# A feed-forward product in seven block products instead of eight, its weight sums made by accumulating DMAs, and the residual kept in DRAM

## The chip, the cores and the metric

The kernel runs on one core of one Trainium2 chip. The metric is the device time of one execution in microseconds (us); less is better. Engines are named as the profile names them: PE (TensorE, the matmuls), DVE (VectorE), ACT (ScalarE), POOL (GpSimd), SP (SyncE, which issues DMAs here).

## What is computed

One layer of a hybrid encoder block on 512 positions plus 16 learned meta positions, with 1024 channels, then a final RMSNorm. The part that the change touches is the feed-forward at the end:

```python
D_MODEL, SEQ, D_FF, FFN_CONV_K = 1024, 512, 2816, 3
...
    h = h + (g_conf * y_conf + g_dn * y_dn) @ w_out
    u2 = rmsnorm(h, norm_ffn_w)
    up = causal_dwconv(u2 @ w_up, ffn_dw_w, ffn_dw_b)
    f_gate, f_val = jnp.split(up, 2, axis=-1)
    return h + (jax.nn.silu(f_gate) * f_val) @ w_down
```

Ahead of it stand a projection `u @ w_in`, a convolution branch, and a gated delta rule with 8 heads in 4 chunks. `u2 @ w_up` has an inner size of 1024 and 5632 output channels: 22 tiles of 128 gate channels and 22 of value channels.

## The kernel before

Everything is float32. A product of full precision is made of three passes: weight and activation are each split into a high part (float32r, a rounded form) and a low part (the rest), and high x high, high x low and low x high are added in PSUM. `weights` loads a 128x1024 weight tile into one of three `wr` buffers by an SP DMA, ACT casts it to `wh`, DVE subtracts to get `wl` (two buffers each). `gemm` issues the matmuls: for 128 output channels and two halves of about 258 positions (256 and two of overlap for the convolution) 8 inner tiles x 3 passes x 2 halves = 48 matmuls of 258 columns.

The stages, in time: the norm and the keys of the heads; the convolution branch; the inverses of the heads' small triangular matrices, which DVE makes in 32x32 blocks and `grow` puts together with 32- and 64-row matmuls on PE (tiles `gP`, `gX`, with `LL` as an operand that POOL clears first); the heads' chunk chains mixed with the products `q`, `v`, `z`, `ga`; the products `y` and `wo`; then the feed-forward. There `up(t)` makes the product of one tile of 128 channels, DVE multiplies it by the norm's reciprocal root `r2` as it leaves PSUM (two instructions of 258 columns), ACT and DVE apply the three taps, ACT the SiLU, DVE multiplies gate by value and both split the result for the second product (tiles `dn`), which starts when the 44th `up` is done. The residual stays in eight SBUF tiles `hs` from `wo` to the end. Big temporary tiles come from a pool of 75 buffers, `bt`.

The order of the instructions of each engine is fixed by a list scheduler that runs when the program is built (`Plan.order`): each recorded operation has a priority (its place in the recording, moved by entries of a table `BIAS`), a modelled cost and its dependencies. Each engine then runs its own list strictly in order and waits at semaphores. So an instruction that waits holds up all behind it on its engine. POOL's list holds only 8 masks (`AFFINE_SELECT`, for tiles `E`) and small `MEMSET`s: of `LL`, and of the four pad columns of `ra`, the copy of `q` or `v` that the short convolution of each head reads. SP issues all DMAs.

Of the kernel before, what the change touches and what calls it, by code (L numbers as in the profile page):

```python
# [36 lines left out]
ROW = T + PAD  # L37

# [82 lines left out]
class Op:  # L121
    _fields = ("eng", "fn", "a", "k", "prio", "deps", "succ", "late", "wait", "cost", "ready", "end", "tiles", "lat", "table", "mode", "act", "tail", "alone")
# [21 lines left out]
TURN = {(False, True): 92, (True, False): 105, (True, True): 190}  # L144
# [6 lines left out]
STAY = 750  # L151
SWITCH = 600

BIAS = {'iv': -1500, 'd0': 100, 'v4': 40, 'v2': 100, 'z1': -570, 't11': -280, 't7': 350, 'k0': -70, 'ln': 250, 's7': -320, 'z0': -700, 'o2': 100, 'o5': 1600, 'd5': -650, 'g3': 150, 'd1': 2160, 'k2': -30, 'q7': -1720, 'k5': -30, 's4': -830, 'w3': -3100, 't2': -670, 'c5': -130, 't8': -40, 'o4': -350, 'q6': 350, 'g4': -350, 't4': -350, 'o1': 250, 'q4': -60, 't9': -750, 'z2': -600, 'o0': -600, 'g0': 30, 'q3': 500, 'q5': 100, 'c6': -30, 's1': -130, 't15': -100, 't1': -730, 's3': -470, 'y0': 250, 't12': -150, 'o6': 700, 'o3': -500, 'k4': -100, 'w2': 250, 't5': -150, 'v0': 30, 'g6': -120, 'z3': 250, 'g5': -190, 'q2': -70, 'y7': -30, 's5': -70, 'v6': -100, 'g1': -250, 'g7': 250, 'm4': 100, 'q0': -250, 'c7': -130, 'd3': -1750, 'o7': 100, 'm6': 30, 'm1': 30, 's6': -100, 'd2': -100, 'y6': 70, 'g2': -600, 'k6': -30, 'z4': -500, 't6': 100, 't3': 250}
LNP = 74
IVP = 1295
UP = 519
WP = 30
# [23 lines left out]

AFTER = 24
# [3 lines left out]
PARTS = (slice(1, 3), slice(0, 1))  # L187

# [9 lines left out]
class Plan:  # L198
# [18 lines left out]
    def add(self, eng, fn, a, k):  # L217
# [28 lines left out]
        if eng == "PE" and fn == "matmul":  # L246

            up = lambda n: 32 if n <= 32 else 64 if n <= 64 else P
            o.mode = (up(args[1].shape[0]), up(writes[0].shape[0]))
            o.mode = None if o.mode == (P, P) else o.mode  # L250
        o.cost, o.lat = self.price(eng, fn, a, k, writes[0])
        o.alone = self.price(eng, fn, a, k, writes[0], True)[0] if o.mode else o.cost
# [11 lines left out]
    def price(self, eng, fn, a, k, out, alone=False):  # L264
        n = out.n
        if eng == "PE":
# [4 lines left out]

            if out.ap.offset // out.tl.row and not alone:
                return 22, 0
# [3 lines left out]
            if lhs.shape[0] == 64:  # L277
                return 115, 0
            return max(n, lhs.n) / 0.6 + 8, 0
        if fn == "dma_start":  # L280
            return 475, int(np.prod(out.shape)) * 4 / 290.0 * (1 if self.run(k) >= P else 2)
# [10 lines left out]
    def order(self):  # L292
# [16 lines left out]
        table, dma, low, done = None, 0.0, 0, bytearray(len(ops))  # L309
        win, act, cold = 0, 0.0, True  # L310
        mode = None
# [14 lines left out]
        def look(e, t):  # L326

            q, nxt, best = ready[e], later[e][0][0] if later[e] else None, None
            for p, i in q:
# [26 lines left out]
                if e == "PE" and mode and o.mode != mode:  # L356
                    p += STAY
                elif o.table and table not in o.table:
                    p += SWITCH
# [4 lines left out]
        while len(out) < len(ops):  # L364
# [26 lines left out]
            if e == "PE":  # L391

                while t >= (win + 1) * WIN:
                    if act < LOW * WIN:
                        cold = True
                    elif act > HIGH * WIN:
                        cold = False
                    win, act = win + 1, 0.0
                if o.mode != mode:
                    c = o.alone + TURN[bool(mode), bool(o.mode)]  # L400
                if cold:
                    c *= 2
                act += o.act * (2 if cold else 1)
                mode = o.mode
            free[e] = t + c
            o.end = free[e]
# [43 lines left out]
def record(A, out):  # L450
# [52 lines left out]
    def gemm(acc, ws, ah, al, ranges, k0=0, kn=None, first=True, last=True):  # L503
# [275 lines left out]
    def decays(h):  # L779
# [54 lines left out]

    ivt = {}
# [350 lines left out]
    r2v = []  # L1186
# [8 lines left out]
    def up(t):  # L1195
# [17 lines left out]
    for t in range(FT):  # L1213
        g = up(t)
# [6 lines left out]
    cuts = ((0, 8), (8, 8), (16, 6))  # L1221

# [5 lines left out]
    for f in range(KT - 1):  # L1228
# [3 lines left out]
        o = hs[f]  # L1232
# [9 lines left out]
    o, s = hs[f], bt(n="fsq")  # L1242
    for b in range(2):
# [50 lines left out]

def _cols(v):
# [43 lines left out]
```

## Time and profile before

| | |
|---|---|
| median of 3 runs | 1037.63 us (1037.09 to 1038.33) |
| the profiled execution, its own time | 1037.14 us, span 1035.4 us, 1.7 us around it |
| PE busy | 1019.7 us, 98% of the span |
| DVE, ACT, POOL busy | 717.1 us, 476.7 us, 8.4 us |
| mean granted TensorE clock | 0.989 of full speed |
| DMA | 98.4 MB, a mean of 95 GB/s |

Busy time is the union of the instructions' own durations. Matmuls overlap (one lasts some 280 ns, the next starts 120 ns after it), so work on PE is counted by start-to-start times, not by durations.

### The profile page before, as it was taken

Reading aid. Unit: us, or ns where it says so; the run is one execution under the profiler, and the core shown is the slowest. Engines: PE = TensorE matmul, PEld = TensorE weight load, DVE = VectorE, ACT = ScalarE, POOL = GpSimd, SP = SyncE. Lnnn points to the kernel's source line nnn. Section 1 sums busy time; section 2 is a strip of 40 time slices with the busy share of each in tenths; the row PEclk is TensorE's granted clock in tenths of the full one; section 3 lists DMA queues with packets and bytes.
Section 4 is the critical chain, followed back from the end, with each engine's and each line's share of the span. In section 5 each row is a group of like instructions: output and inputs, shape, how many; then the busy total and the mean of one; then the engine's idle time right before and its main releaser. Section 6 shows DMA issues by size and latency. Waiting matters only on the chain.

```text
span 1035.4 us, 20014 instructions
## 1 busy us (share of the span) xinstructions
PE 1019.7 (98%) x8430; PEld 978.8 (95%) x8430; DVE 717.1 (69%) x1237; ACT 476.7 (46%) x847; POOL 8.4 (1%) x45
## 2 busy tenths in 40 slices
PE   9999999998999999999999999999999999999996
PEld 7999999998999999999999999999999999988886
DVE  5985699996599999996266555667676767623323
ACT  5787622446645565453254233544444444422222
POOL 0000000000000000000000000000000000000000
PEclk9999999997999999999999999999999999999998
DMA  6143333241121241214214332222222222333332
GB/s 220 63 135 93 100 108 111 83 123 52 43 97 54 67 132 54 93 62 144 82 42 153 115 121 82 86 100 83 101 86 99 82 103 84 95 92 92 97 92 82
DMA packets 44042, 98.40 MB, mean 95 GB/s; under 512 B 12720, under 2 KB 19248, under 8 KB 43952
## 3 DMA queue, kind: packets, MB, share of 16 engines
q1 hardware_dynamic: 43952, 97.12, 28.7%
q8 instruction: 66, 1.08, 0.4%
q14 instruction: 24, 0.20, 0.1%
HBM read 93.89 MB, written 3.21 MB: 94 GB/s over the span
## 4 chain that ended last, share of the span: by engine, by line
PE 92%; DVE 3%; ACT 3%; DMA 1%; issue 1%; SPq 0%; POOL 0%; DVEq 0%; ACTq 0%; POOLq 0%
PE up L447 25%; PE dn L447 12%; PE ga L447 9%; PE y L447 9%; PE z L447 5%; PE v L447 5%; PE wo L447 5%; PE q L447 4%; PE cv L447 4%; PE cg L447 3%; PE k L447 2%; PE o L447 2%; PE rs L447 1%; PE S L447 1%; PE wP L447 1%; DVE cv L447 1%
## 5 line engine op out<-in xcount | busy, mean ns | idle before, releaser
L447 DVE TENSOR_TENSOR wl<-wr,wh 128x1024 fp32r<-128x1024 f32 x157 | 189.3, 1206 | 156.7 <-PE dn L447 59.8
L447 ACT CAST wh<-wr 128x1024 fp32r<-128x1024 f32 x157 | 162.6, 1037 | 250.2 <-PE dn L447 57.5
L447 DVE SCALAR_TENSOR_TENSOR ca<-c,par,ca 128x516 f32<-128x516 f32 (+13 forms) x240 | 175.5, 742 | 3.1 <-ACT ca L447 0.3
L447 PE MATMUL up<-hh,wh 128*128 128x258 f32 x704 | 141.6, 282 | 0.0
L447 PE MATMUL up<-hl,wh 128*128 128x258 f32 x704 | 141.3, 282 | 0.0
L447 PEld LDWEIGHTS up<-hh,wh 128*128 128x128 f32 x704 | 109.2, 190 | 0.2 <-issue 0.2
L447 PEld LDWEIGHTS up<-hl,wh 128*128 128x128 f32 x704 | 108.7, 189 | 0.0
L447 PE MATMUL up<-hh,wl 128*128 128x258 f32 x704 | 91.9, 283 | 0.0
L447 PEld LDWEIGHTS up<-hh,wl 128*128 128x128 f32 x704 | 87.5, 190 | 0.0
L447 PE MATMUL dn<-fh,wh 128*128 128x512 f32 (+1 forms) x198 | 71.7, 370 | 0.0
L447 PE MATMUL dn<-fl,wh 128*128 128x512 f32 (+1 forms) x198 | 71.2, 368 | 0.0
L447 DVE SCALAR_TENSOR_TENSOR uy<-up,par,uy 128x512 f32<-128x512 f32 x88 | 65.9, 749 | 2.8 <-ACT uy L447 1.3
L447 DVE TENSOR_TENSOR up<-up,r 128x258 f32<-128x258 f32 x88 | 33.5, 420 | 47.1 <-PE up L447 44.3
L447 ACT ACTIVATE uy<-up,par 128x512 f32<-128x512 f32 x44 | 35.9, 816 | 55.4 <-DVE up L447 55.4
L447 PE MATMUL ga<-uh,wh 128*128 128x258 f32 (+1 forms) x256 | 56.9, 287 | 0.0
L447 PE MATMUL ga<-ul,wh 128*128 128x258 f32 (+1 forms) x256 | 56.6, 288 | 0.0
L447 DVE SCALAR_TENSOR_TENSOR cv<-ra,par,cv 128x528 f32<-128x528 f32 x69 | 51.3, 759 | 0.2
L447 PE MATMUL dn<-fh,wl 128*128 128x512 f32 (+1 forms) x198 | 45.4, 369 | 0.0
L447 PE MATMUL ga<-uh,wl 128*128 128x258 f32 (+1 forms) x256 | 44.6, 289 | 0.0
L447 PEld LDWEIGHTS dn<-fh,wh 128*128 128x128 f32 x198 | 37.2, 188 | 7.0
L447 PEld LDWEIGHTS dn<-fl,wh 128*128 128x128 f32 x198 | 37.2, 188 | 6.6
L447 PEld LDWEIGHTS ga<-uh,wh 128*128 128x128 f32 x256 | 42.1, 190 | 0.2
(284 smaller groups left out, 2195.9 us busy)
## 6 DMA issues: line engine op xcount, KB each, us to landing
wr<-in_win SPq DMA_DIRECT2D x64, 512.0 KB
wr<-in_wup SPq DMA_DIRECT2D x44, 512.0 KB
wr<-in_wd SPq DMA_DIRECT2D x17, 512.0 KB
wr<-in_wdn SPq DMA_DIRECT2D x8, 512.0 KB
wr<-in_wco SPq DMA_DIRECT2D x8, 512.0 KB
wr<-in_wo SPq DMA_DIRECT2D x8, 512.0 KB
wr<-in_wd SPq DMA_DIRECT2D x8, 384.0 KB
x<-in_xT SPq DMA_DIRECT2D x8, 264.0 KB
```

The source lines that it names most:

```text
L447: getattr(engines[o.eng], o.fn)(*(get(x) for x in o.a), **{n: get(x) for n, x in o.k.items()})
```

## The change

The feed-forward's first product is made for 3 of its 22 tile pairs (gate tile t and value tile t) as before. The other 19 pairs, called blocks here, are each a 2x2 block product: two halves of the inner size, two halves of the output channels (gate, value), two halves of the positions. `seven` makes it with seven block products in place of eight, in Winograd's form, which shares sums: each product has 4 inner tiles x 3 passes = 12 matmuls of 258 columns, and the seven accumulate in two PSUM regions X and Z whose running value is taken out between products (`quarters`: four takes by ACT, three by DVE).

- The sums of activations are made once, by `factors`, for the four pairs of inner tiles, right after `r2`: DVE first multiplies the residual by norm weight and `r2` (tiles `xn`; so the blocks need no multiplication by `r2` later), makes the sums (`nt`, `nq`) and splits all seven operands (`nh`, `nl`, `nhl`).
- The sums of weights are made by `presums` in DRAM, one 1 MB tile `ws` for each block: POOL issues two copies DRAM to DRAM of 512 KB and three accumulating DMAs (512, 256 and 256 KB). Accumulating ones wait for those before. Two blocks are under way at a time, and the first waits for the last mask.
- Each block's weights come in 3 loads of 512 KB and one of 256 KB, each split by ACT and DVE, in place of two of 512 KB.
- The residual is stored to DRAM (`d_h`, 8 DMAs of 256 KB) and read back tile by tile (`hr`) in the second product. This and three `iv` buffers for the last products make room in `bt`.
- The scheduler's model of PE and of DMAs is changed and the table `BIAS` is other throughout, so the order differs in all stages.

```diff
-STAY = 750
-SWITCH = 600
...
+STAY = 1920
+SWITCH = 300
...
-WP = 30
+WP = 144
...
+NPRE = 3
...
+    def presums(src, n, hold):
+        r = [plan.tile("dram", "con", [P, 4, HD], F32, "ws") for _ in range(n)]
+        for m in range(n):
+          with plan.at(1):
+            h = {hold} | ({softs[-2]} if len(softs) > 1 else set())
+            plan.after = set(h)
+            G.dma_start(out=r[m][:, 0:2], in_=src[:, m, 0:3:2])
+            plan.after = set(h)
+            G.dma_start(out=r[m][:, 2:4], in_=src[:, m, 0:2])
+            G.dma_start(out=r[m][:, 1:3], in_=src[:, m, 3:4].broadcast_to([P, 2, HD]), accum_op=ALU.add)
+            G.dma_start(out=r[m][:, 0], in_=r[m][:, 1], accum_op=ALU.add)
+            G.dma_start(out=r[m][:, 3], in_=r[m][:, 0], accum_op=ALU.add)
+            softs.append(len(plan.ops) - 1)
+        return r
+    def seven(src, m, sums, B, w, use):
+        acc = p2("se")
+        X, Z = acc[:, 0, :w], acc[:, 1, :w]
+        flat = lambda v: v.rearrange("p b c -> p (b c)")
+        tiles = (flat(src[:, m, 0:2]), flat(sums[m][:, 0:2]), flat(sums[m][:, 2:4]), src[:, m, 2])
+        for i, (b, to, first, what) in enumerate((('b11', X, True, 'p1'), ('b21', Z, True, 'c11b'),
+                                                  ('t2', X, False, 'u2'), ('t1', Z, True, 'c22b'),
+                                                  ('t3', X, False, 'u3'), ('b22', Z, False, 'c12b'),
+                                                  ('t4', X, False, 'c21'))):
+            if i % 2 == 0:
+                with plan.at("sw"):
+                    hi, lo = weights(tiles[i // 2], D if i < 6 else HD)
+            n, c = len(B), i % 2 * HD
+            runs = [(k, x, y) for part in PARTS for k in range(n) for x, y in ((lo, 0), (hi, 0), (hi, 1))[part]]
+            for j, (k, x, y) in enumerate(runs):
+                PE.matmul(to, lhsT=x[:, c + k * P:c + (k + 1) * P], rhs=B[k][b][y], start=first and j == 0, stop=j == len(runs) - 1,
+                          skip_group_check=not first)
+            use(what, to)
+    def quarters(src, m, sums, B, w, n):
+        c = [bt(n=n), bt(n=n)]
+        q = lambda i, j: c[i][:, j * w:(j + 1) * w]
+        def use(what, acc):
+            i, j = {'p1': (0, 0), 'u2': (0, 1), 'c22b': (1, 1), 'c21': (1, 0),
+                    'c11b': (0, 0), 'c12b': (0, 1), 'u3': (1, 1)}[what]
+            if what in ('p1', 'u2'):
+                S.copy(out=q(i, j), in_=acc)
+            elif what in ('c22b', 'c21'):
+                S.mul(out=q(i, j), in_=acc, mul=-1.0)
+            else:
+                V.tensor_tensor(out=q(i, j), in0=q(i, j), in1=acc, op=ALU.subtract if i else ALU.add)
+        seven(src, m, sums, B, w, use)
+        return c
+    def factors(x0, x1, w, n, hold=None):
+        q = 2 * (w + 2)
+        sub = lambda t: t[:, :q].rearrange("p (b w) -> p b w", b=2)[:, :, :w]
+        two = lambda t: t[:, :2 * w].rearrange("p (b w) -> p b w", b=2)
+        t = bt(n=n + "t")
+        X0, X1, TT = two(x0), two(x1), two(t)
+        hold = set() if hold is None else {hold}
+        plan.after = set(hold)
+        V.tensor_tensor(out=TT[:, 0], in0=X0[:, 0], in1=X0[:, 1], op=ALU.subtract)
+        V.tensor_tensor(out=X0[:, 1], in0=X1[:, 1], in1=X0[:, 1], op=ALU.subtract)
+        V.scalar_tensor_tensor(out=TT[:, 1], in0=TT[:, 0], scalar=-1.0, in1=X1[:, 1], op0=ALU.mult, op1=ALU.subtract)
+        t4 = bt(n=n + "q")
+        V.scalar_tensor_tensor(out=t4[:, :w], in0=TT[:, 1], scalar=-1.0, in1=X1[:, 0], op0=ALU.mult, op1=ALU.subtract)
+        r = {}
+        for v, names in ((X0, ('b11', 't3')), (X1, ('b21', 'b22')), (TT, ('t1', 't2'))):
+            hi, lo = bt(F32R, n + "h"), bt(F32R, n + "l")
+            plan.after = set(hold)
+            S.copy(out=sub(hi), in_=v)
+            V.tensor_tensor(out=sub(lo), in0=v, in1=sub(hi.bitcast(F32)), op=ALU.subtract)
+            for b, nm in enumerate(names):
+                r[nm] = (sub(hi)[:, b], sub(lo)[:, b])
+        hl = bt(F32R, n + "hl")
+        S.copy(out=sub(hl)[:, 0], in_=t4[:, :w])
+        V.tensor_tensor(out=sub(hl)[:, 1], in0=t4[:, :w], in1=sub(hl.bitcast(F32))[:, 0], op=ALU.subtract)
+        r['t4'] = (sub(hl)[:, 0], sub(hl)[:, 1])
+        return r
 
...
+    wus = presums(A['wuq'], FT - NPRE, masks[-1])
...
+    d_h = [con([P, SEQ], "d_h", "dram") for _ in range(KT)]
+    for f in range(KT):
+        SY.dma_start(out=d_h[f], in_=hs[f][:, 4:TW])
...
+        for f in range(0, KT, 2):
+            with plan.at(f"h{f}"):
+                ab = []
+                for i in range(2):
+                    x = bt(n="xn")
+                    for b in range(2):
+                        V.scalar_tensor_tensor(out=x[:, b * 258:(b + 1) * 258], in0=hs[f + i][:, 2 + 256 * b:260 + 256 * b],
+                                               scalar=pc('nf', f + i), in1=r2v[b], op0=ALU.mult, op1=ALU.mult)
+                    ab.append(x)
+                ub.append(factors(*ab, 258, "n"))
...
+    def ffn(t):
+        if t < NPRE:
+            g, v = up(t), up(NPRE + t)
+        else:
+            g, v = quarters(A['wuq'], t - NPRE, wus, ub, 258, "up")
+        with plan.at("tp" if t < NPRE else "tq"):
+            ends(t, g, v)
+    def ends(t, g, v):
+        g = taps3(g, t)
         S.activation(out=g[:, :SEQ], in_=g[:, :SEQ], func=AF.Silu)
-        v = up(FT + t)
+        v = taps3(v, FT + t)
         V.tensor_tensor(out=g[:, :SEQ], in0=g[:, :SEQ], in1=v[:, :SEQ], op=ALU.mult)
-        a, b = split(g[:, :SEQ], SEQ, "f")
+        if t < FT - 3:
+            a, b = split(g[:, :SEQ], SEQ, "f")
+        else:
+            hl = plan.tile("sb", "iv", [P, D], F32R, "fv")
+            a, b = hl[:, :SEQ], hl[:, SEQ:]
+            S.copy(out=a, in_=g[:, :SEQ])
+            V.tensor_tensor(out=b, in0=g[:, :SEQ], in1=a.bitcast(F32), op=ALU.subtract)
         fh.append(a)
         fl.append(b)
+    for t in range(FT):
+        call(ffn, "u", t)
...
+    def back(f):
+        o = bt(n="hr")
+        SY.dma_start(out=o[:, 4:TW], in_=d_h[f])
+        hr.append(o)
+        return o
 
...
-        o = hs[f]
+        o = back(f)```

Counted over the whole program, PE has 228 matmuls of 258 columns less (2112 in the first product before; 288 `up` and 1596 `se` now). DVE has 19 weight splits of 1024 and 19 of 512 columns more, 76 `up` multiplications less and 57 takes from PSUM more, and 48 instructions around `factors`. ACT has the same weight casts more, 76 takes from PSUM and 16 casts in `factors`. POOL has 95 DMAs more.

**PE, middle of the first product.** Before, `up` is one product after the other, and each weight tile serves two matmuls in a row (x2: the two halves of positions; `hh`, `hl` are the parts of the activation):

```order
L447 MATMUL up_8718<-hl_7769,wh_8634 128x258 x2
L447 MATMUL up_8718<-hh_7822,wh_8634 128x258 x2
L447 MATMUL up_8718<-hl_7832,wh_8634 128x258 x2
L447 MATMUL up_8718<-hh_7885,wh_8634 128x258 x2
L447 MATMUL up_8718<-hl_7895,wh_8634 128x258 x2
```

Now, early in the blocks, two blocks' accumulators (`se_8520`, `se_8588`) take turns, and weights change at each matmul:

```order
L469 MATMUL se_8520<-nl_8227,wh_8640 128x258
L469 MATMUL se_8588<-nh_8231,wh_8652 128x258
L469 MATMUL se_8520<-nh_8292,wl_8655 128x258
L469 MATMUL se_8588<-nl_8250,wh_8652 128x258
L469 MATMUL se_8520<-nh_8373,wl_8655 128x258
L469 MATMUL se_8588<-nh_8327,wl_8669 128x258
L469 MATMUL se_8520<-nh_8458,wl_8655 128x258
```

So while a region waits to be taken out of PSUM, PE can have a product of the neighbouring block to run.

**DVE, from `r2` on.** Before, the takes of `up` alternate with taps (`uy`) and weight splits (`wl`):

```order
L447 RECIPROCAL rr_7999<-rr_7999 128x129
L447 TENSOR_TENSOR up_8043<-up_7925,r_1_8033 128x258 x2
L447 SCALAR_TENSOR_TENSOR uy_8056<-up_8043,par_69,uy_8056 128x512
L447 TENSOR_TENSOR up_8073<-up_7968,r_1_8033 128x258
L447 SCALAR_TENSOR_TENSOR uy_8056<-up_8043,par_69,uy_8056 128x512
L447 TENSOR_TENSOR up_8073<-up_7968,r_1_8033 128x258
L447 TENSOR_TENSOR wl_8089<-wr_7878,wh_8045 128x1024
```

Now the factors follow `r2`, and the taps come after them:

```order
L469 RECIPROCAL rr_8129<-rr_8129 128x129
L469 TENSOR_TENSOR up_8173<-up_8053,r_1_8163 128x258 x2
L469 SCALAR_TENSOR_TENSOR xn_8183<-xr_7516,par_82,r_1_8163 128x258 x2
L469 SCALAR_TENSOR_TENSOR xn_8195<-xr_7560,par_82,r_1_8163 128x258 x2
L469 TENSOR_TENSOR nt_8205<-xn_8183 128x258
L469 TENSOR_TENSOR up_8212<-up_8098,r_1_8163 128x258
L469 TENSOR_TENSOR xn_8183<-xn_8195,xn_8183 128x258
L469 SCALAR_TENSOR_TENSOR nt_8205<-nt_8205,xn_8195 128x258
L469 TENSOR_TENSOR nl_8227<-xn_8195,nh_8209 128x2x258
```

From the first take after `r2` to the split of the first block's weights (`wl_8541`) DVE's list now has 10 takes of `up`, 16 products `xn`, 8 sums each as TENSOR_TENSOR and as SCALAR_TENSOR_TENSOR of 258 columns, 12 splits of 2x258, 4 of 258 and 4 weight splits.

**POOL.** Before, its list after the last mask holds only clearings:

```order
L447 AFFINE_SELECT E_1484<-E_1484 128x512
L447 MEMSET ra_2326 128x4
L447 MEMSET ra_2547 128x4
L447 MEMSET LL_2994 32x8x32
L447 MEMSET LL_3000 32x8x32
```

Now 29 DMAs stand between the last mask and the first clearing of `LL`, the last of them here:

```order
L469 DMA ws_2481<-in_wuq 128x2x512
L469 DMA ws_2530<-in_wuq 128x2x512
L469 DMA ws_2481<-ws_2481 128x512
L469 DMA ws_2530<-ws_2530 128x512
L469 DMA ws_2481<-ws_2481 128x512
L469 MEMSET LL_2476 32x8x32
L469 MEMSET LL_2485 32x8x32
```

Clearings now stand behind DMAs that wait for other DMAs; 93 of the 95 DMAs stand ahead of the last one (`ra_5659`).

## Rows read from the trace of the kernel before

**Rows 1.** The page: busy time, share and instructions of each engine.

```profile
span 1035.4 us, 20014 instructions
PE 1019.7 (98%) x8430; PEld 978.8 (95%) x8430; DVE 717.1 (69%) x1237; ACT 476.7 (46%) x847; POOL 8.4 (1%) x45
```

**Rows 2.** Stretches: length, busy time (instructions) by engine, granted clock, DMA share, GB/s.

```profile
200.00:300.00 100.00, 96.05 (x1079) 92.95 (x1078) 76.19 (x134) 54.48 (x134) 0.95 (x7) 0.93 0.26 78
300.00:400.00 100.00, 100.00 (x858) 95.97 (x856) 97.59 (x155) 57.19 (x124) 0.77 (x9) 1.00 0.25 83
700.00:800.00 100.00, 100.00 (x836) 100.00 (x835) 68.90 (x105) 40.92 (x52) 0.00 (x0) 1.00 0.27 93
```

**Rows 3.** Instructions on tile `up`: duration min/median/max in ns, first and last start.

```profile
L447 PE MATMUL up<-hh,wh x704: 278/282/390, 644.8 to 897.5; 128*128 128x258 f32 x176
L447 PE MATMUL up<-hh,wl x704: 278/282/287, 648.9 to 899.7; 128*128 128x258 f32 x176
```

**Rows 4.** Timeline of PE where two products alternate: start, duration.

```profile
223.11 0.28 PE L447 MATMUL v<-uh,wl 128*128 128x264 f32 x1
223.23 0.28 PE L447 MATMUL ga<-uh,wh 128*128 128x260 f32 x1
```

**Rows 5.** Groups by shape, DVE and ACT: busy us, mean ns, idle before.

```profile
L447 DVE TENSOR_TENSOR wl<-wr,wh 128x1024 fp32r<-128x1024 f32 x149 | 181.7, 1219 | 141.5 <-PE dn L447 48.4 <-ACT wh L447 34.3 <-PE y L447 19.4
L447 DVE SCALAR_TENSOR_TENSOR uy<-up,par,uy 128x512 f32<-128x512 f32 x88 | 65.9, 749 | 2.8 <-ACT uy L447 1.3
L447 DVE TENSOR_TENSOR up<-up,r 128x258 f32<-128x258 f32 x88 | 33.5, 420 | 47.1 <-PE up L447 44.3 <-ACT r L447 2.8
L447 DVE TENSOR_TENSOR fl<-uy,fh 128x512 fp32r<-128x512 f32 x22 | 15.2, 692 | 29.3 <-ACT fh L447 29.3
L447 DVE SCALAR_TENSOR_TENSOR hl<-xr,par,hh 128x516 fp32r<-128x516 f32 x8 | 6.1, 757 | 6.4 <-ACT hh L447 6.4
L447 ACT CAST wh<-wr 128x1024 fp32r<-128x1024 f32 x149 | 156.0, 1048 | 245.9 <-PE dn L447 53.3 <-PE up L447 45.6 <-PE y L447 30.6
L447 ACT COPY r<-rc 128x258 f32<-128x258 f32 x2 | 0.7, 374 | 3.3 <-PE rc L447 3.3
```

**Rows 6.** Timeline of DVE where it is full: start, duration.

```profile
340.74 0.76 DVE L447 SCALAR_TENSOR_TENSOR cv<-ra,par,cv 128x528 f32<-128x528 f32 x1
341.41 0.74 DVE L447 SCALAR_TENSOR_TENSOR ca<-c,par,ca 128x501 f32<-128x501 f32 x1
```

**Rows 7.** Timeline of DVE at the first use of `r2`.

```profile
655.98 0.76 DVE L447 TENSOR_TENSOR up<-up,r 128x258 f32<-128x258 f32 x2 [2.82 <-ACT r L447]
```

**Rows 8.** Half a microsecond inside a weight load of 512 KB, columns as in rows 2.

```profile
760.00:760.50 0.50, 0.50 (x7) 0.50 (x5) 0.00 (x0) 0.50 (x2) 0.00 (x0) 1.00 0.95 385
```

**Rows 9.** SP's timeline: DMAs through DRAM and the next that reads them.

```profile
130.02 0.38 SPq L447 DMA_DIRECT2D d_mm<-Mm  x1
...
132.35 0.29 SPq L447 DMA_DIRECT2D iv<-d_mm  x1
...
217.08 0.38 SPq L447 DMA_DIRECT2D d_x<-XT  x1
...
222.42 3.51 SPq L447 DMA_DIRECT2D DU<-d_x  x4
```

**Rows 10.** POOL's last mask, and ACT's last copy into `ra`.

```profile
115.41 0.63 POOL L447 TENSOR_SCALAR_AFFINE_SELECT E<-E 128x512 f32<-128x512 f32 x1 [14.74 <-DMA E<-d_g]
...
L447 ACT COPY ra<-v x8: 579/600/609, 193.1 to 431.2; 128x528 f32<-128x528 f32 x8
```

**Rows 11.** Stretches around `grow`, columns as in rows 2.

```profile
230.00:240.00 10.00, 8.74 (x211) 8.26 (x209) 9.61 (x17) 8.32 (x30) 0.38 (x3) 1.00 0.16 56
240.00:250.00 10.00, 7.93 (x66) 7.55 (x67) 5.49 (x9) 6.96 (x19) 0.00 (x0) 0.58 0.16 54
250.00:260.00 10.00, 10.00 (x122) 9.46 (x120) 3.71 (x9) 4.47 (x11) 0.10 (x1) 0.74 0.08 27
```

**Rows 12.** SP's own waits: what for, us in total, times, longest.

```profile
SPq L447 <- DVE wl L447: 708.3, 130, 15.3
```

More of the change, by code (lines that the diff above doesn't have):

```diff
@@ L121 @@
 class Op:
-    _fields = ("eng", "fn", "a", "k", "prio", "deps", "succ", "late", "wait", "cost", "ready", "end", "tiles", "lat", "table", "mode", "act", "tail", "alone")
+    _fields = ("eng", "fn", "a", "k", "prio", "deps", "succ", "late", "wait", "cost", "ready", "end", "tiles", "lat", "table", "mode", "act", "tail", "part", "size")
 class Rec:
@@ L187, with __init__, run @@
 PARTS = (slice(1, 3), slice(0, 1))
+class Array:
+    def __init__(self):
+        self.win, self.act, self.cold, self.mode, self.drain, self.tiles = 0, 0.0, True, None, 0.0, {}
+    def run(self, o, t):
+        while t >= (self.win + 1) * WIN:
+            if self.act < LOW * WIN:
+                self.cold = True
+            elif self.act > HIGH * WIN:
+                self.cold = False
+            self.win, self.act = self.win + 1, 0.0
+        x = 2 if self.cold else 1
+        self.act += o.act * x
+        if o.mode != self.mode:
+            t = max(t, self.drain) + (INTO * x if o.mode and not self.mode else 0)
+            self.mode, self.tiles = o.mode, {}
+        if not o.mode:
+            return t + o.cost * x, t + o.cost * x
+        t = max(t, self.tiles.get(o.part, 0.0))
+        n, m = o.size
+        self.tiles[o.part] = t + PART * (n + m) * x
+        end = t + (PART * n + OUTOF) * x
+        self.drain = max(self.drain, end)
+        return t + 7 * x, end
 def hit(a, b):
@@ L250, in add @@
             o.mode = None if o.mode == (P, P) else o.mode
+            o.part = (args[1].ap.offset // args[1].tl.row, writes[0].ap.offset // writes[0].tl.row)
+            o.size = (args[2].n, max(args[1].n, args[1].shape[0]))
         o.cost, o.lat = self.price(eng, fn, a, k, writes[0])
-        o.alone = self.price(eng, fn, a, k, writes[0], True)[0] if o.mode else o.cost
         o.act = (args[2].n if writes[0] is args[0] else args[1].n) / 0.6 * o.mode[0] / P if o.mode else o.cost
@@ L270, in price @@
                 return 110, 0
-            if out.ap.offset // out.tl.row and not alone:
-                return 22, 0
             if lhs.tl.dt == F32R:
                 return RATE * n + 4 + (2 if rhs.ap.offset % rhs.tl.row % 4 else 0), 0
-            if lhs.shape[0] == 64:
-                return 115, 0
             return max(n, lhs.n) / 0.6 + 8, 0
         if fn == "dma_start":
+            if eng == "POOL":
+                return 1000, int(np.prod(out.shape)) * 4 / 140.0
             return 475, int(np.prod(out.shape)) * 4 / 290.0 * (1 if self.run(k) >= P else 2)
@@ L308, in order @@
             heapq.heappush(line[v.tag], (v.first, id(v), v))
[L309 to L311 removed]
+        table, dma, soft, low, done = None, 0.0, 0.0, 0, bytearray(len(ops))
+        array = Array()
         for i, o in enumerate(ops):
@@ L355, in look @@
                     continue
-                if e == "PE" and mode and o.mode != mode:
+                if e == "PE" and array.mode and o.mode != array.mode:
                     p += STAY
@@ L391, in order @@
             if e == "PE":
[L393 to L406, printed above, removed]
+                free[e], o.end = array.run(o, t)
+            else:
+                free[e] = o.end = t + c
             if e == "SP":
-                dma = max(dma, t + 950) + o.lat
+                dma = max(dma, t + 1350) + o.lat * (1.5 if soft > t else 1)
                 o.end = dma + o.tail
+            elif o.fn == "dma_start":
+                soft = max(soft, t + 2000) + o.lat
+                o.end = soft + 1500
             out.append(i)
@@ L1200, in up, with taps3 @@
         u = bt(n="up")
+        for b in range(2):
+            V.tensor_tensor(out=u[:, b * 258:(b + 1) * 258], in0=acc[:, b, :258], in1=r2v[b], op=ALU.mult)
+        return u
+    def taps3(u, t):
         uv = halves(u[:, :516], 258)
-        for b in range(2):
-            V.tensor_tensor(out=uv[:, b], in0=acc[:, b, :258], in1=r2v[b], op=ALU.mult)
         y = bt(n="uy")
```

37 lines of the change are left out of this document (24 added, 13 removed).

## The prediction

> **What bounds the kernel now.** I read the page first, then the stretches, then tile `up`, then DVE and POOL where the change puts work. PE is busy for 1019.7 of 1035.4 us [rows 1], so only work taken from PE, or PE's few idle places, can shorten the end. In the stretches PE is full from 300 us on at full clock, and in the feed-forward it starts 836 matmuls in 100 us, one per 0.1196 us [rows 2]; DVE is busy for 69% there and DMA moves 93 GB/s. The first product runs from 644.8 to about 899.8 us [rows 3]: 255.0 us for 2112 matmuls, 0.1207 us each with the few small ones of `r2` between them. I use 0.120. Where two products alternate and the weights change at every matmul, the starts are 0.12 us apart too [rows 4], so the new order with alternating blocks costs PE nothing in itself. The places where PE lost time are around `grow`: between 230 and 260 us it was idle for 1.3 and 2.1 us, and the granted clock fell to 0.58 and 0.74 [rows 11], that is to the 1.2 GHz level for part of the time, after stretches of 32-row matmuls and waits.
>
> **The sum, part by part.** It is made against the profiled execution, 1037.14 us (span 1035.4 and 1.7 around it); the median of the runs is 0.5 us above it.
>
> *PE's saving.* Each block has 7 x 12 = 84 matmuls where there were 96. 19 blocks x 12 = 228 fewer, x 0.120 = **-27.4 us**. A block now lasts 84 x 0.120 = 10.1 us.
>
> *The opening.* The factors can't start before `r2`, whose first use on DVE is at 656.0 us [rows 7], 11.2 us after the first `up`. What DVE must then do until the first block's low weights are ready is listed with the change. Prices: a take of 258 columns lasts 0.420, one of 512 lasts 0.692, a SCALAR_TENSOR_TENSOR of 516 lasts 0.757, a weight split 1.219 us [rows 5]. In a full DVE one instruction starts 0.08 us before the end of the last (0.76 long, the next 0.67 later [rows 6]), so each costs its duration less 0.08. The trace has no SCALAR_TENSOR_TENSOR of 258 columns; it lies between 0.42 (the take) and 0.757, and I take 0.48, the one of 516 less 258 columns at the 1.07 ns per column between 0.420 and 0.692. So: 22 TENSOR_TENSORs of 258 x 0.34 = 7.5; 24 x 0.40 = 9.6; 12 splits of 516 x 0.62 = 7.4; 4 weight splits x 1.14 = 4.6; together 29.1 us, to 685.1 us. PE by then has 6 x 48 = 288 matmuls of `up` and 13 of the first block that need no low weights: 644.8 + 301 x 0.120 = 680.9 us. PE waits for the difference and a handoff of some 0.3 us: **+4.5 us** (2 if ACT and DVE hand over without gaps and the factors' sums come at 0.34; 8 if each of the 12 splits waits for its cast on ACT, an idle of 0.3 us).
>
> *The stream of blocks.* DVE per block: 3 weight splits of 1024, 3.66, one of 512, 0.69; three takes, 1.26; four taps at 0.749, 3.00; gate by value and the split, 1.38: 9.99 us of durations, and with 13 overlaps of 0.08 less, **8.95 us** against PE's 10.1. So DVE goes from 69% to 88% in steady state, plus the taps of the first three pairs, which now come late (18 instructions, about 12 us). 19 x 8.95 + 12 = 182 us stand against 19 x 10.1 = 192: it fits, with 10 us to spare. ACT has 3 casts at 1.048, one at half, four takes near 0.374 (the copy of 258 columns from PSUM), taps and SiLU and cast near 2.9: about 8 of 10.1 us. What can cost PE is a take that comes late: a region must be emptied while the other product runs, 12 x 0.120 = 1.44 us, and a weight split of 1.14 us in front of a take of 0.34 uses all of it. From both sides: nothing, as where DVE was 97.6% busy from 300 to 400 us and PE still had no idle [rows 2]; at most DVE's full durations plus two handoffs of 0.3 us, 10.6 us per block, which is 0.5 x 19 = 9 us. I take **+3 us**, nearer to the row of 97.6%, because neighbouring blocks alternate there too.
>
> *Loads.* A block loads 3 x 512 + 256 KB = 1.8 MB in 10.1 us, 181 GB/s against 93 now. Inside a load the rate is 385 GB/s [rows 8], and SP's time is mostly spent waiting for a `wr` buffer (708.3 us in 130 waits [rows 12]). The three buffers turn over every 8.7 us, in which a load of some 2 us, a cast and a split fit. **0**, covered by that wait; without cover each load would cost its 2 us.
>
> *The residual's way through DRAM.* 16 DMAs of 256 KB, 0.7 us each at 385 GB/s, stand between loads on SP. A store waits for the tile that `wo` makes, and the next load is queued behind it. Both lie in the same wait for a buffer: **0**; uncovered, 16 x 0.7 = 11 us.
>
> *POOL's list.* Nothing in the trace is a DMA from POOL or an accumulating one. Nearest rows: 8 KB through DRAM take 2.3 us from issue to the reader's issue, 512 KB into DRAM 5.3 us [rows 9]. With two blocks interleaved, and 385 GB/s behind a landing of 2.3 us, ten DMAs take some 17.5 us, 1.75 each. If each waited for the one before at 5.3 us for 512 KB and 3.8 for 256, five take 23.5, 4.7 each. With those landings and interleaving, a pair takes 9.4 (four copies) + 6.7 + 4.5 + 4.5 = 25 us, **2.5 us each**, which I take. The time there is: the last mask is at 115.4 us and the last copy into `ra` at 431.2 [rows 10], and 93 DMAs lie between: 316 / 93 = 3.4 us each. So the clearings come in time, and the weight sums long before their blocks. **0** on the path.
>
> *The other order ahead of 640 us.* PE's matmuls there are the same. At best the losses around `grow` go: 3.4 us idle, and at 0.58 and 0.74 some 84% and 52% of 10 us ran at half clock, 13.6 / 2 = 6.8 us. `grow` keeps its runs of small matmuls, and as much could be lost anew. **0**, from -8 to +8.
>
> Sum: 1037.14 - 27.4 + 4.5 + 3 = 1017.2, and 0.5 for the median: **1017.5 us**.
>
> **The rivals.** One: *DVE paces the blocks*. For it: 8.95 of 10.1 us, in a fixed list with waits on ACT and PE in both directions. Against it: the full stretch at 300 us, which fed PE. If each of three takes on DVE comes 0.3 us late in each block, 57 x 0.3 = 17 us: 1037.6 - 27.4 + 4.5 + 17 = **1032 us**. It eats the whole gain from 0.4 us per take.
>
> Two, the one on the other side: *POOL's DMAs come late and hold the clearings*. POOL runs in order, so a late DMA delays every clearing behind it, then ACT's copy into `ra` or `grow`'s operand, then PE, whose list can't skip. At 4.0 us per DMA the last clearing would be at 115 + 93 x 4 = 487 us, 56 us late, against 20 us gained: **1074 us**. It decides from (316 + 20) / 93 = 3.6 us each. For it: 3.6 lies between my 2.5 and the 4.7 of the upper bound, an accumulating DMA also reads its destination, and DMA has a share of 0.25 already [rows 2]. Against: two blocks overlap. The Trainium skill ("SBUF — State Buffer", section "SBUF: two separate sides") names a way to this end: while DVE runs a copy in its two-port mode, GpSimd can't write the descriptors of its own DMAs, and they wait for DVE. By its wording plain `tensor_tensor` work has no such mode, and DVE's large groups here are TENSOR_TENSOR and SCALAR_TENSOR_TENSOR [rows 5], so by that rule little should happen; no run here shows a DMA from POOL yet.
>
> Three: *more than the count*. The new order also removes the losses at `grow`: 1017.5 - 8 = **1009 us**. For it only the dip in rows 11; against it that `grow`'s small matmuls remain.
>
> Four: *nothing moves*, because the opening, the takes and a slip on POOL add up to the saving: within 2 us of 1037.6.
>
> **How the numbers follow.** The likeliest, 0.60, ends between 1009 and 1026 (opening 2 to 8, blocks 0 to 9, order -8 to +8, which will not all fall on one side). Rival one 0.14, two 0.16, three 0.06, four 0.04. Two runs differ by up to 0.12%, so 0.2%, or 2 us, is what can be told from no change: faster 0.80, same 0.04, slower 0.16. Leaving out most of rival two above 1040 and the far end of three below 1006 leaves about 0.2 outside: **1006 to 1040 us**.
>
> **What the changed profile would show.** PE: 1596 `se` matmuls, starts 0.12 us apart, from the first to the last some 195 us; ahead of them a gap of about 4.5 us in which PE waits for DVE's `nl` or `wl`. DVE near 90% busy there, DMA near 180 GB/s. POOL: the last of the 93 DMAs issued before 430 us, less than 3.4 us apart, and no wait of ACT or PE for POOL. The forecast is wrong if PE waits for takes in every block (rival one), if `ra` or `LL` waits for POOL (two), or if the stages ahead of 640 us end more than 8 us away from where they did.

## The result: slower by 5.65%

The changed kernel takes 1096.47 us (median of 4 runs, 1093.5 to 1097.96) where the kernel before takes 1037.36 (1037.02 to 1038.33): a ratio of 1.0565, 95% interval 1.054 to 1.0589. The forecast was 1017.5 us. The profiled execution has a span of 1093.8 us against 1035.4 [rows 1]. The page of the changed kernel, busy times:

```profile
span 1093.8 us, 20102 instructions
PE 1021.3 (93%) x8202; PEld 957.6 (88%) x8202; DVE 768.7 (70%) x1304; ACT 537.2 (49%) x975; POOL 88.5 (8%) x140
```

PE has 228 matmuls less, as worked out, and is idle for 72.5 us where it was idle for 15.7. Where, the stretches say (columns as in rows 2):

```profile
200.00:300.00 100.00, 95.47 (x1090) 91.40 (x1089) 75.92 (x116) 52.37 (x119) 23.28 (x39) 0.97 0.81 184
300.00:400.00 100.00, 100.00 (x876) 98.20 (x875) 96.75 (x144) 48.08 (x87) 24.60 (x35) 1.00 0.85 192
700.00:800.00 100.00, 81.09 (x588) 73.00 (x589) 73.90 (x106) 56.88 (x91) 0.00 (x0) 1.00 0.42 134
```

Ahead of the feed-forward little has changed, though the DMA share has risen from 0.25 to 0.8. In the blocks PE starts 588 matmuls in 100 us in place of 836, at full clock, and neither DVE nor ACT is full: this is waiting, not work. The bounds of the stages, from the instructions on `up` and `se` (columns as in rows 3):

```profile
L469 PE MATMUL up<-hh,wh x96: 276/282/384, 652.4 to 685.9; 128*128 128x258 f32 x96
...
L469 PE MATMUL se<-nl,wh x456: 276/283/393, 689.5 to 954.3; 128*128 128x258 f32 x152
...
L469 PE MATMUL se<-nhl,wl x76: 276/280/295, 710.6 to 957.8; 128*128 128x258 f32 x76
```

The first product runs from 652.4 to 957.9 us, 305.5 in place of 255.0 [rows 3]: +50.5. It starts 7.6 later, and what follows it lasts 0.3 longer: together the 58.4 us between the spans. The 19 blocks take 268 us, 14.1 each; 10.1 was expected. Who waits for the takes (tile `up`: waiting engine and tile, us, times):

```profile
who waited for it (us, times):
  PEld se L469: 66.4, 100
  PE se L469: 45.6, 96
```

And one such wait, from the timelines of PE and of ACT (start, duration, idle before and its end):

```profile
804.49 0.28 PE L469 MATMUL se<-nh,wh 128*128 128x258 f32 x1
804.61 0.28 PE L469 MATMUL se<-nl,wh 128*128 128x258 f32 x1
805.35 0.39 PE L469 MATMUL se<-nh,wh 128*128 128x258 f32 x1 [0.47 <-ACT up L469]
...
804.92 0.38 ACT L469 COPY up<-se 128x258 f32<-128x258 f32 x1 [0.18 <-PE se L469]
```

PE has begun a product, starts two matmuls of it, stands for 0.47 us, and goes on 0.05 us after a take ends. That take, in turn, starts when the second of these matmuls ends (804.61 + 0.28 = 804.89), though it reads the product before. PE and the take wait for each other in turn: one start is 0.74 us after the last in place of 0.12.

### The profile page after: what moved, and what is told of

Its sections match the earlier page's. It is cut to its first block, busy times and chain, and to the rows that moved or that the text cites. A ratio compares the mean times of both kernels' runs of the same rounds, so it can differ in the third digit from the quotient of the medians.

```text
span 1093.8 us, 20102 instructions
## 1 busy us (share of the span) xinstructions
PE 1021.3 (93%) x8202; PEld 957.6 (88%) x8202; DVE 768.7 (70%) x1304; ACT 537.2 (49%) x975; POOL 88.5 (8%) x140
## 3 DMA queue, kind: packets, MB, share of 16 engines
q1 hardware_dynamic: 51728, 116.26, 33.5%
## 4 chain that ended last, share of the span: by engine, by line
PE 75%; DVE 13%; DMA 5%; ACT 4%; issue 2%; SPq 0%; DVEq 0%; ACTq 0%
PE se L469 19%; PE dn L469 11%; PE y L469 8%; PE ga L469 6%; PE wo L469 4%; PE q L469 4%; PE z L469 4%; PE v L469 3%; PE cg L469 2%; DVE up L469 2%; DVE wl L469 2%; ACT up L469 2%; PE cv L469 2%; DMA orb<-d_r 2%; PE k L469 1%
## 5 line engine op out<-in xcount | busy, mean ns | idle before, releaser
L469 DVE TENSOR_TENSOR wl<-wr,wh 128x1024 fp32r<-128x1024 f32 (+2 forms) x195 | 225.4, 1159 | 200.3 <-ACT wh L469 65.5
L469 ACT CAST wh<-wr 128x1024 fp32r<-128x1024 f32 (+2 forms) x195 | 194.2, 997 | 271.0 <-PE dn L469 57.1
L469 DVE SCALAR_TENSOR_TENSOR ca<-c,par,ca 128x516 f32<-128x516 f32 (+12 forms) x240 | 175.4, 745 | 3.8 <-ACT ca L469 0.2
L469 PE MATMUL se<-nh,wh 128*128 128x258 f32 x456 | 120.2, 296 | 23.4 <-ACT up L469 13.5
L469 PE MATMUL se<-nl,wh 128*128 128x258 f32 x456 | 117.7, 290 | 13.7 <-ACT up L469 6.9
L469 PEld LDWEIGHTS se<-nh,wh 128*128 128x128 f32 x456 | 83.8, 189 | 34.6 <-ACT up L469 20.6
L469 PEld LDWEIGHTS se<-nl,wh 128*128 128x128 f32 x456 | 83.4, 189 | 19.8 <-ACT up L469 10.4
L469 PE MATMUL se<-nh,wl 128*128 128x258 f32 x456 | 77.0, 283 | 0.8 <-ACT up L469 0.8
L469 PEld LDWEIGHTS se<-nh,wl 128*128 128x128 f32 x456 | 64.9, 190 | 1.2 <-ACT up L469 1.2
L469 DVE SCALAR_TENSOR_TENSOR uy<-up,par,uy 128x512 f32<-128x512 f32 x88 | 63.7, 746 | 3.0 <-ACT uy L469 2.9
L469 PE MATMUL dn<-fh,wh 128*128 128x512 f32 (+1 forms) x171 | 61.9, 370 | 0.0
L469 PE MATMUL dn<-fl,wh 128*128 128x512 f32 (+1 forms) x171 | 61.6, 368 | 0.0
L469 POOL DMA_DIRECT2D ws<-in_wuq x57 | 48.6, 881 | 156.0 <-DMA ws<-in_wuq 80.0
L469 PE MATMUL ga<-uh,wh 128*128 128x258 f32 (+1 forms) x256 | 58.1, 292 | 0.6 <-ACT gt L469 0.6
L469 DVE TENSOR_TENSOR up<-up,se 128x258 f32<-128x258 f32 x57 | 24.0, 423 | 48.1 <-PE se L469 45.8
L469 PE MATMUL ga<-ul,wh 128*128 128x258 f32 (+1 forms) x256 | 57.1, 290 | 0.0
L469 DVE SCALAR_TENSOR_TENSOR cv<-ra,par,cv 128x528 f32<-128x528 f32 x69 | 50.5, 756 | 0.1
L469 PEld LDWEIGHTS ga<-uh,wh 128*128 128x128 f32 x256 | 42.3, 191 | 1.8 <-ACT gt L469 0.8
L469 POOL DMA_DIRECT2D ws<-ws x38 | 34.9, 924 | 100.0 <-DMA ws<-in_wuq 53.1
L469 PEld LDWEIGHTS ga<-ul,wh 128*128 128x128 f32 x256 | 42.2, 192 | 0.3 <-issue 0.2
L469 PE MATMUL ga<-uh,wl 128*128 128x258 f32 (+1 forms) x256 | 41.9, 290 | 0.0
L469 PE MATMUL dn<-fh,wl 128*128 128x512 f32 (+1 forms) x171 | 39.7, 369 | 0.0
## 6 DMA issues: line engine op xcount, KB each, us to landing
wr<-in_win SPq DMA_DIRECT2D x64, 512.0 KB
ws<-in_wuq POOLq DMA_DIRECT2D x57, 512.0 KB, 7.9
wr<-ws SPq DMA_DIRECT2D x38, 512.0 KB
ws<-ws POOLq DMA_DIRECT2D x38, 256.0 KB, 6.4
wr<-in_wuq SPq DMA_DIRECT2D x19, 512.0 KB
wr<-in_wd SPq DMA_DIRECT2D x17, 512.0 KB
wr<-in_wuq SPq DMA_DIRECT2D x19, 256.0 KB
wr<-in_wdn SPq DMA_DIRECT2D x8, 512.0 KB
```

Source lines behind the costliest of these rows:

```text
L469: getattr(engines[o.eng], o.fn)(*(get(x) for x in o.a), **{n: get(x) for n, x in o.k.items()})
```

## Theories

**A, the shared tile.** X and Z are the two halves of one tile `se`. The planner keeps its books by regions (`hit` compares boxes), and so plans that Z is filled while X is taken. The waits in the finished list go by the whole tile: a matmul into Z that stands behind X's take waits for it, and the take waits for the matmuls into Z ahead of it. **B**: the takes are late because ACT and DVE are behind. **C**: a matmul stands while another engine reads the accumulator memory, whatever tile. In the list of PE, block `se_9751`, the second product (into Z) shows what A says; it has all its operands, and waits for ACT at its sixth matmul (one list entry per line):

```
L469 MATMUL se_9751<-nh_8292,wh_9727 128x258
L469 MATMUL se_9751<-nl_8306,wh_9727 128x258
L469 MATMUL se_9751<-nh_8373,wh_9727 128x258
L469 MATMUL se_9751<-nl_8398,wh_9727 128x258
L469 MATMUL se_9751<-nh_8458,wh_9727 128x258
L469 MATMUL se_9751<-nl_8484,wh_9727 128x258 [waits Activation_49]
```

What it waits for is ACT's take of X of this block, and that take in its turn waits for the fifth of these matmuls into Z, not for the last one into X. Of 187 waits of the 1596 `se` matmuls, 98 stand at neither the first matmul of a product nor the first one with low weights.

## Experiments on the blocks

**Two tiles for X and Z** (called *apart* below).

```diff
-        acc = p2("se")
-        X, Z = acc[:, 0, :w], acc[:, 1, :w]
+        X, Z = p1("sx")[:, :w], p2("sz")[:, 0, :w]
```

> The seven products of a block go into two tiles, one for X and one for Z, instead of into the two halves of one tile; nothing else is written differently. Theory A: in the changed kernel a matmul into one half waits for the take of the other half, because both are one tile, and the take waits for the matmuls into the other half that stand ahead of it; that is the 14.1 us per block instead of 10.1. Then the first product `se` to the last take some 195 to 205 us instead of 268, the waits of PE's weight loads on `up` under 10 us instead of 63.7, and the time 1020 to 1030 us. Theory B (the takes come late because ACT and DVE are behind with casts and splits): the same waits in other places, over 1080 us. Theory C (a matmul stands still while another engine reads the accumulator memory, whatever tile): 1090 us, unchanged.

Measured: 1022.26 us, ratio to before 0.9841 (0.9816 to 0.9867). In the list 2 of 175 waits are left inside a product. A stretch inside the blocks, the last matmuls of the first product, and who waits for `up`:

```profile
700.00:800.00 100.00, 98.53 (x817) 98.06 (x816) 95.86 (x140) 74.89 (x123) 0.00 (x0) 1.00 0.55 181
```

```profile
L469 PE MATMUL sx<-nhl,wl x76: 276/282/287, 706.2 to 884.6; 128*128 128x258 f32 x76
```

```profile
who waited for it (us, times):
...
  PEld sx L469: 1.1, 2
  PE sx L469: 0.7, 2
```

A holds: 66.4 us of waiting become 1.1. B falls: DVE is fuller than in the changed kernel (95.9 of 100 us against 73.9), and the takes come in time. C falls: as many takes, of the same size, are made beside running matmuls. One thing is not parted: the planner's lists are the same up to the first product, but from there *apart* has an order of its own on PE, DVE and ACT, so what the waits for takes don't cover of the gain may be the order's. The Trainium skill ("PSUM — Partial Sum Buffer", section "Summary: rules for kernel authors") asks for waits by bank, so that one bank may be read while a matmul runs into another; each half of `se` has 512 float32, which the same page (section "Specifications (TRN2)") gives for a bank. This run agrees: with a tile for each half the waits between them are gone, and the time falls by 74.2 us.

**Both in small tiles**, one bank each.

```diff
+        X, Z = p1("sx")[:, :w], p1("sz")[:, :w]
```

> X and Z in two tiles of one bank each, from the four that the norms use, and none of the two wide ones. Theory A: as the run with two tiles to within 4 us, since only the parting of the tiles matters. If the number of accumulators in flight matters beside it, over 5 us slower, as the norms and the fourth tile then compete.

Measured: 1023.0 us, 0.9832 (0.9785 to 0.9878): as *apart*. The parting is what matters, not which buffers.

**Every second block apart.**

```diff
+        if m % 2:
+            X, Z = p1("sx")[:, :w], p2("sz")[:, 0, :w]
+        else:
+            acc = p2("se")
+            X, Z = acc[:, 0, :w], acc[:, 1, :w]
```

> X and Z in one tile in the 10 blocks of even number and in two tiles in the 9 of odd number. If each block of one tile costs the same for itself, (1096.5 - 1022.3) / 19 = 3.9 us, the time is 1022.3 + 10 x 3.9 = 1061 us (1056 to 1066). If the waits of one block are worked off in the next, or only a row of such blocks runs late, clearly less, 1025 to 1045.

Measured: 1063.8 us, 1.0254 (1.0239 to 1.0269): (1063.8 - 1022.3) / 10 = 4.2 us per block of one tile, against (1096.5 - 1022.3) / 19 = 3.9 with all of them. Each pays for itself.

## Experiments on the sums in DRAM

*Apart* still begins the first product at 651.2 us, 6.4 later than before.

**Without the sums' DMAs, in one tile and in two.**

```diff
-    wus = presums(A['wuq'], FT - NPRE, masks[-1])
+    wus = [None] * (FT - NPRE)
...
-        tiles = (flat(src[:, m, 0:2]), flat(sums[m][:, 0:2]), flat(sums[m][:, 2:4]), src[:, m, 2])
+        tiles = (flat(src[:, m, 0:2]), flat(src[:, m, 1:3]), flat(src[:, m, 2:4]), src[:, m, 2])
```

> As the run with two tiles, and without the 93 DMAs that make the weight sums: the second and third weight of each block are read from the unsummed quarters, in the same sizes, so the sums are left out. Theory A1 (the DMAs of GpSimd's queue cost the 7.5 us by which the first product of the feed-forward starts later): first `up` near 645 and 6 to 9 us less than the run with two tiles. Theory A2 (the other order ahead costs them): within 2 us of the run with two tiles.

> The changed kernel with its one tile for X and Z, without the 93 DMAs that make the sums (left out as in the run before). If the stall of the stream of blocks is the shared tile alone, it stays: 14 us per block and 1085 to 1092 us. If the loads of the sums from DRAM, or their queue, had slowed the stream, it falls towards 10 us per block, 1015 us.

Measured: 1018.67 us, 0.9808 (0.9775 to 0.9841), in two tiles; 1090.51, 1.051 (1.0481 to 1.054), in one. The stall stays without the sums, as A says. In two tiles that is 3.6 us less than *apart*, which is neither A1 (6 to 9) nor A2 (within 2). What the DMAs cost these two can't tell: without them the planner writes another order for all engines, and that order has a loss of its own (two tiles, stretch 500 to 550 us: PE 44.85 of 50 us at a clock of 0.93; *apart* has 49.32 at 1.00).

**The same order, the DMAs not sent.** The plan is made with them, and they are left out when it is written down. A second part of the edit, not shown, lets the loads read as many bytes of unsummed weights, in this run and the next.

```diff
+                if o.eng == "POOL" and o.fn == "dma_start":
+                    continue
```

> The version with two tiles, every engine's instructions in exactly its order, but the 95 DMAs of GpSimd's queue are planned and then not sent (the sums are left out; the loads read as many bytes of unsummed weights). Theory U1 (the DMAs cost what is lost ahead of the feed-forward: PE had 353 and 397 matmuls in 150 to 200 and 100 to 150 us against 413 and 408 before): 410 or so in both, first `up` at 645 to 646, and 5 to 7 us less than the version with two tiles, 1015 to 1017. Theory U2 (the other order costs it, the DMAs nothing): within 2 us of that version, 1020 to 1024.

Measured: 1004.34 us, 0.9685 (0.9671 to 0.97). The DMAs cost time, as U1 says, but I had it three times too small: 18 us less than *apart* and not 5 to 7, and the first product starts at 635.2 us and not at 645. Tile `up` and the stretches, first without the DMAs:

```profile
L471 PE MATMUL up<-hh,wh x96: 276/282/384, 635.2 to 668.7; 128*128 128x258 f32 x96
```

```profile
100.00:200.00 100.00, 99.92 (x820) 99.04 (x819) 72.06 (x209) 47.23 (x117) 2.70 (x9) 1.00 0.37 110
200.00:300.00 100.00, 99.77 (x1149) 95.61 (x1148) 87.45 (x137) 55.79 (x128) 0.54 (x6) 1.00 0.21 70
```

then *apart*:

```profile
L469 PE MATMUL up<-hh,wh x96: 276/283/384, 651.2 to 684.7; 128*128 128x258 f32 x96
```

```profile
100.00:200.00 100.00, 93.40 (x748) 92.12 (x747) 69.34 (x208) 44.18 (x113) 21.72 (x27) 0.97 0.87 209
200.00:300.00 100.00, 96.28 (x1102) 92.25 (x1101) 76.05 (x116) 51.96 (x118) 25.20 (x40) 0.98 0.81 189
```

The DMAs cost 651.2 - 635.2 = 16.0 us ahead of the first product, and the other order by itself gains 644.8 - 635.2 = 9.6: it has 1149 matmuls in 200 to 300 us against 1079 [rows 2], with the clock at 1.00 in place of 0.93. A place where the DMAs bite is the read-back of the inverses, 4 DMAs `DU<-d_x`. ACT's timeline in *apart*:

```profile
191.54 0.69 ACT L469 COPY mn<-DU 32x128 f32<-32x128 f32 x3 [6.70 <-DMA DU<-d_x]
194.13 1.30 ACT L469 COPY mn<-DU 32x128 f32<-32x128 f32 x5 [1.91 <-DMA DU<-d_x]
195.46 0.61 ACT L469 ACTIVATE ct<-cg 128x528 f32<-128x528 f32 x1
```

They were issued from 176.2 to 179.1 us; the last lands 15 us after that. `ct` stands behind these copies on ACT, and PE waits 4.7 us for `ct`:

```profile
PE q L469 <- ACT ct L469: 4.7, 1, 4.7
```

With no sums sent the same copies wait for no DMA:

```profile
182.75 2.01 ACT L471 COPY mn<-DU 32x128 f32<-32x128 f32 x8
184.78 0.61 ACT L471 ACTIVATE ct<-cg 128x528 f32<-128x528 f32 x1
```

**An eighth of their columns.** Same order again.

```diff
+                if o.eng == "POOL" and o.fn == "dma_start":
+                    get = lambda v: (v.make()[:, :, :64] if len(v.shape) == 3 else v.make()[:, :64]) if isinstance(v, Vw) else v
```

> As the run in which the DMAs of the sums are not sent, but they are sent with an eighth of their columns (the sums are left out), with as many DMAs and rows of 256 bytes for 2048. If their bytes on the DMA engines cost the loss ahead of the feed-forward, the time is that of the run that sends none, within 1.5 us; if it is the number of DMAs, their queue and GpSimd's clearings behind them, it is that of the version with two tiles.

Measured: 1005.02 us, 0.969 (0.9674 to 0.9707): as with none sent, though 5.0 MB of the 39.9 MB still go. The 95 issues, their descriptors and their places in POOL's list cost nothing that shows; the size of the transfers does.

**Starting later.** Three ways: a later hold in the plan; a copy on POOL that reads the inverses; one that reads the first head's output.

```diff
+    wus = presums(A['wuq'], FT - NPRE, len(plan.ops) - 1)
...
+        gt0 = con([P, 1], "gt0")
+        G.tensor_copy(out=gt0, in_=ivt['DU'][:, 0, 0:1])
...
+        G.tensor_copy(out=gt0, in_=st_h[h][:, T0:T0 + 1])
```

> The version with two tiles, with the first DMA of the sums held until the inverses' result has been read back from DRAM (some 210 us) instead of until the last mask (110 us). If U1 holds and the loss comes through the small transfers of the inverses, which wait for DMA engines that the sums fill, PE keeps its 410 matmuls in both stretches and the time falls by 3 to 6 us, to 1016 to 1019; if the same loss comes wherever the DMAs lie, or the order costs it, it stays at 1020 to 1024.

> The version with two tiles and a true wait: GpSimd copies one column of the inverses' result, which comes back from DRAM, before its first DMA, so that no DMA of the sums is on the engines before some 180 us (the hold tried before set only an order, and the trace shows DMAs from 100 us on). Theory U3 (the bytes cost time mainly in 100 to 250 us, 397, 353 and 696 matmuls against 414, 409 and 736 with the DMAs not sent, 113 x 0.12 = 13.6 us; the stretches 250 to 400 lose nothing at 80 to 90% DMA share): 1008 to 1013 us. Theory U4 (they cost wherever they lie): 1018 to 1024.

> As the version whose sums wait for the inverses, but the wait is on the first head's output, so that the DMAs lie in some 270 to 620 us instead of 180 to 530. Theory U3: nothing lost at the inverses and the heads' starts, 1006 to 1011 us. U4: 1018 to 1024. A third way: the later DMAs collide with the loads after 450 us, 3 to 8 us slower than with the wait on the inverses.

Measured: 1027.26 us, 0.9906 (0.9891 to 0.992); 1030.09, 0.9929 (0.9908 to 0.9949); 1024.55, 0.9882 (0.9835 to 0.9928). None gained; the first two lie outside what either theory gave, the third just above U4's range. The first shows that a hold in the plan is an order and not a wait: the DMA share is 0.79 in 100 to 150 us. The other two did keep their early stretches clean (411 matmuls in 100 to 150 us in both) and lost it at 500 to 550 us (PE 41.26 and 44.42 of 50, clock 0.86 and 0.90). But each has an order of its own again, so they don't decide between U3 and U4; my sum from two stretches was not enough for a forecast.

**One chain of DMAs, the order of all others kept.** The plan is *apart*'s; when it is written down, the sums go into POOL's list block by block, one DMA every 5.6 us of planned time; in the second run one every 4.7 us, with a start meant to be 100 us later.

```diff
+            line = [i for i in range(len(self.ops)) if soft(i)]
+            rest = [i for i in seq if not soft(i)]
...
+                while k < len(line) and (o.at >= t0 + k * 5600 or need and any(j in o.deps for j in line[k:])):
+                    seq.append(line[k])
+                    k += 1
```

> The version with two tiles, PE, DVE, ACT and SP in exactly its order; only GpSimd's list changes: the sums are made block by block, one chain of DMAs at a time in place of two side by side, spread over some 110 to 640 us in place of 110 to 450. Theory U5 (the loss of 18 us comes from how full the DMA engines are, 0.8 to 0.9 there): their share falls to 0.5 to 0.65, and a part of the 18 us comes back, 1008 to 1016 us. Theory U4 (each byte of the sums costs PE the same wherever it lies): 1020 to 1024 us. A third way, over 1024: GpSimd's clearings come late behind a chain that waits.

> As the run with one chain, but the first DMA stands 100 us later in GpSimd's list, behind the clearings of the inverses' stage (some 210 us), and the chain ends near 650 us. If the transfers of the inverses are what the sums delay (in 150 to 250 us PE had 1049 matmuls with the sums, 1145 without), 1006 to 1012 us. If the share of the engines alone counts, as the run with one chain, within 3 us.

Measured: **1006.81 us, 0.9704 (0.9686 to 0.9722)**, and 1010.05, 0.9728 (0.9706 to 0.9751). The stretches with one chain:

```profile
100.00:200.00 100.00, 99.92 (x819) 99.04 (x819) 71.63 (x208) 47.15 (x115) 18.64 (x27) 1.00 0.75 188
200.00:300.00 100.00, 99.73 (x1149) 95.56 (x1148) 87.84 (x138) 55.59 (x127) 15.14 (x24) 1.00 0.58 137
```

All bytes are still moved, and PE has its 819 and 1149 matmuls: 15.5 of the 18 us are back. U4 falls, since the bytes cost little with this spread. U5 holds in kind, but the gain is larger than I had put it (1008 to 1016), at a share that fell less (0.69 from 110 to 592 us, where 0.5 to 0.65 was expected). Two things came together here, one chain in place of two and the spread over 481 us in place of 346, and no run parts them. Nor does the later start decide between the share of the engines and the transfers of the inverses: in neither run is a wait of a copy put down to the read-back `DU<-d_x`. In the second the five DMAs of the first block still ran from 112.6 us, since nothing made them wait, and the others followed from 231.7 us; it is 3.2 us slower, and its first product starts 4.3 us later. The first of the two beats both kernels.

## Why the prediction was wrong, step by step

- **PE's saving, -27.4: held**, once the tiles are apart. *Apart*'s first product runs from 651.2 to 884.7 us (its last matmul starts at 884.6), 233.5: 21.5 less than 255.0, so 5.9 of the saving is lost inside it.
- **The opening, +4.5, and the stream, +3:** together 7.5, against these 5.9 in *apart*. The load on DVE and DMA was sized well (from 690 to 880 us DVE is busy for 91.9%, and DMA moves 181 GB/s), and so was DVE's work of the opening: in the changed kernel 28.4 us from the first use of `r2` to the first block's low weights, against 29.1. But the gap ahead of the blocks isn't there: PE waits there for 1.2 us, and 0.3 more in the changed kernel, where 4.5 was forecast. *Apart* loses 2.2 us more in three waits inside the blocks; I haven't assigned the rest, so that the sum came close is partly luck.
- **The stream as changed: the step that failed.** The prediction says "a region must be emptied while the other product runs, 12 x 0.120 = 1.44 us": here the other product doesn't run. The term was 3, bounded by 9; it measured 305.5 - 233.5 = 72.0 us more than with two tiles, of which the difference in waits of weight loads for `up` is 65.3; I have not assigned the other 6.7. Rival one was at the right place, the takes, with the wrong mechanism and a fourth of the price: DVE paced nothing (73.9 of 100 us busy). The rows that I showed of the list (two blocks taking turns) were from the start of the blocks, and without their waits. The same list with waits, further on, has 98 of them inside products; no row of the kernel before could show it, since there both halves of a tile were taken only when both were done.
- **POOL's list, 0 on the path: failed, 16.0 us.** The 95 DMAs took 345 us (110.7 to 455.3), 3.6 each; I had 2.5, and 3.6 as the point of decision. In the changed kernel (columns as in rows 3):

```profile
L469 POOL DMA_DIRECT2D ws<-in_wuq x57: 538/947/1218, 110.7 to 442.7; - x57
L469 POOL DMA_DIRECT2D ws<-ws x38: 802/818/1360, 129.3 to 455.3; - x38
```

So they were as slow as rival two needed, but its mechanism wasn't there: in the changed kernel no wait from 100 to 640 us is put down to a clearing of POOL; other transfers landed late. I priced the DMAs as a queue and not as a load on what the stage ahead moves. From 111 to 456 us the share is 0.84. The rule that the prediction weighed (the Trainium skill, "SBUF — State Buffer", section "SBUF: two separate sides", GpSimd's descriptors behind DVE's two-port copies) changed nothing here, as its wording for `tensor_tensor` work had it: with an eighth of the columns the 95 DMAs cost 0.7 us, within the spread of the runs.
- **The other order ahead, 0 from -8 to +8: -9.6**, rival three's mechanism (from 200 to 300 us PE is idle for 0.2 us at a clock of 1.00 without the sums, where it was idle for 4.0 at 0.93), which the sums took back.
- **Loads and residual, 0: held.** From the last first-product matmul to the end it is 135.6 us before and 134.9 in *apart*, which moves 181 GB/s in the blocks.

Together: -21.5 + 72.0 + 16.0 - 9.6, 1.2 by which the changed kernel's first product starts later than *apart*'s (the lists ahead of it are the same), and 0.3 at the end: 58.4 us, the difference of the spans. Each term is from one profiled execution of each kernel.

## What to carry to other kernels

Two regions that are filled and emptied in turn need a tile each, if the waits are made by tile: read the order with its waits, in the steady state, and ask of each wait inside a run of one accumulator what it is for. A side stream of DMAs is costed by what it does to the transfers of the stage that it runs beside, and one chain of them, spread further, cost less here than two packed closely (2.5 us against 18). When a part is taken out to price it, keep the order of everything else: with the same DMAs left out, two orders differed by 14 us (1018.67 and 1004.34).

## What the hardware showed beside that

DMAs from DRAM to DRAM were slower than my upper bounds of 5.3 and 3.8 us, with two chains side by side: 7.9 us to landing for 512 KB, 6.4 for 256 KB, in the median of the changed kernel. The 57 are 38 plain copies and 19 accumulating ones, the 38 are all accumulating (its page, DMA issues):

```profile
ws<-in_wuq POOLq DMA_DIRECT2D x57, 512.0 KB, 7.9
...
ws<-ws POOLq DMA_DIRECT2D x38, 256.0 KB, 6.4
```

And PE lost nothing to being read beside: in *apart*, from 750 to 800 us, it starts 418 matmuls in 50 us, as before the change (836 in 100 [rows 2]), while three takes by DVE and four by ACT leave its accumulators in each block.
